# Dilated layer of a two-layer trunk: filler moved from between the weighted sums to between projection, scores, maxima and exponentials of the first head pairs

## The chip, the cores and the metric

The kernel runs on one core of one Trainium2 chip. The metric is device microseconds of one execution of the whole program. Lower is better. A core has TensorE (PE, matmuls and transposes), VectorE (DVE), ScalarE (ACT), GpSimd (POOL) and SyncE (SP, which issues the loads here). "PEld" in a profile is TensorE's loading of the stationary operand, and "PEclk" is the clock that TensorE was granted, as a share of its full 2.4 GHz; the lower of its two levels, 1.2 GHz, reads as 0.50.

## What is computed

The reference is a trunk of two layers over 512 tokens of width 1024. Layer 0 has stick-breaking attention, layer 1 dilated attention; each is followed by a feed-forward block of width 4096 and a gated side input. The change is in the dilated attention alone:

```python
proj = (x @ w_in).reshape(B, S, G, 3, H, HEAD_DIM)        # G = 3 groups, H = 8 heads of 64
for g, (window, dil) in enumerate(((128, 1), (512, 4), (2048, 16))):
    q, k = rope(proj[:, :, g, 0]), rope(proj[:, :, g, 1]); v = proj[:, :, g, 2]
    o, lse = banded_attention(strided(q), strided(k), strided(v), window // dil)
alpha = softmax(stack(lses), axis=0)                       # weights of the three groups
o = einsum('gbsh,gbshd->bshd', alpha, stack(outs))
return o @ w_out
```

All is in 32-bit floats. A product is made of three matmuls on rounded parts (high by high, high by low, low by high).

## The kernel before: how the work is tiled and ordered

**The work of one head pair.** Heads are taken two at a time: pairs 0 to 3. For each pair and each group g there is a *query job* `queries(pr, g)` (L691): the q projection, 8 *steps* of three 128x512 matmuls, then the k projection, 8 steps more. When the last step of a half is reached, its result is turned by the rotary tables on VectorE (L698 to L705: a shuffle, two products, a sum), and after the k half both are split in a rounded high part (ACT) and a low part (VectorE), `qh, ql, kh, kl` (L264, L266). `scores(pr, g)` (L714) is 24 small matmuls, with a masked copy and running maximum of each block on VectorE (L735). When all three groups are scored, `maxima` (L738) transposes the maxima (L743, L745), combines them on ACT and VectorE, and transposes them back (L757); `exps` (L764) makes 16 exponentials on ACT in place in the score tiles `S` (L774). In this document "M-out" is the first set of transposes (L743) and "M-back" the second (L757). Then `attend` (L826) runs the weighted sums: 8 `turn`s (L781: up to four transposes of exponentials, and a split in `th` on ACT, L799, and `tl` on VectorE, L800), 8 `apply`s (L807: matmuls of the values V with th and tl, L820), one `divide` (16 matmuls, L844 and L847, and four reciprocals, L852), and the combination (L874 to L877). Four turns run ahead of the applies.

**The filler.** The order on TensorE is the order in which the program is written out; the other engines are ordered by a planner from priorities (`due`, for instance rope ahead of the split of q and k, that ahead of the scores' copies, those ahead of `tl`). To keep TensorE busy while other engines work, query jobs, and later the values' projection of the last two pairs (`values`, steps of six matmuls), are not run in one piece: they lie in a queue (`Filler`, L118), and the program takes steps from it. `fill(t)` takes steps until their nominal costs (0.65 for a step of a query job, 0.72 for one of the values) cover t; a remainder is carried over. `fill.until(label, then)` takes steps until the job `label` is finished and `then` more of the nominal clock is past. All steps have to run once, so a step that is taken in one place is missing in another.

**Where steps are taken.** The loop over the pairs (L932 to L944) is:

```python
for pr in range(4):
    while pieces and pieces[0][0] == pr:
        fill.until(pieces[0][:2], TUNE["lag"])
        piece()                              # scores of (pr, g)
        fill(TUNE["pgap"])
    fill(TUNE["m0"])
    N = maxima(MM[pr])                       # holds fill(TUNE["m1"]) between M-out and M-back
    late, DD[pr] = exps(SS[pr], N)
    fill(TUNE["m2"])
    if pr < 2:
        attend([pr], TUNE["gap"])
```

Within `attend`, `tick(gap)` (L928) follows each turn ahead and each apply: it takes steps worth `gap`, and then runs the scores of the next pair's next group if its job has been finished for `lag`. So pairs 0 and 1 each have an attend of their own, in which the scores of the next pair lie; pairs 2 and 3 are attended together at the end with their own constant `gap2`, when the queue is empty.

**Buffers.** Tiles of 128x512 come from one pool of 42 (`acts`, L172): the layer's input (16), the rotary tables (2), the four parts of each query job until its scores are done, the eight score tiles of a pair until they have been turned, and the two parts of each pair's output. Score results and turns come from six banks of PSUM (`wb`), projections from two (`mmb`).

Of the kernel before, what the change touches and what calls it, by code (L numbers as in the profile page):

```python
# [25 lines left out]
TUNE = dict(late=4, gap2=1.0, hik=1, lok=0, sqk=1, pieces=4, of=5, og=4, warm=9, wprep=0, s1a=-400, s1b=200, e=25,  # L26
            oev=25, qev=-400, hsplit=-200, vev=50, rope=-800, ttr=-100, exps=200, turn=-50, maxi=-50, comb=-100,
            norm=400, res=-400, resk=2, yev=-50, fev=25, gate=0, fin=-50, fe=2.0, ff=0.0, fg=5.0, qlag=5.0, fa=0.57,
            fb=0.32, slope=0.05, lag=8.0, gap=1.2, m0=6.0, m1=5.5, m2=8.0, p0=5.0, p1=2.0, p2=8.0, hp0=6, hp1=30,
            hps=2, blag=1.5, vlag=0.0, fx=5.5, ahead=4, pgap=0.0, vev1=50)  # L30
NUNIT = 220
BIG = float(2.0 ** 100)
GAINS = ("g_mix_pre", "g_mix_post", "g_ffn_pre", "g_ffn_post", "g_ple")
# [132 lines left out]
def program(tc, ctx, w_dram, x_dram, xs_dram, p_dram, pos_dram, g_dram, c_dram, out_dram):  # L166
# [475 lines left out]
    def dilated(xh, xl, sq, oh, ol, partial, out, prepare):  # L642
        swap = list(range(8, 16)) + list(range(8)) + list(range(16, 32))
        with tc.tile_pool(name="dlw", bufs=1, reuse_waits="tile") as wp:
# [93 lines left out]
            def maxima(M):  # L738

                dve.tensor_max(M[:, 1], M[:, 1], M[:, 2])  # L740
                r0, r1 = wide(), wide()
                for i in range(4):
                    pe.transpose(r1[0:2, i * P:(i + 1) * P], M[:, 1, i, :], ident)  # L743
                for i in range(4):
                    pe.transpose(r0[0:2, i * P:(i + 1) * P], M[:, 0, i, :], ident)  # L745
                fill.clock += 0.9
                m1, m0 = tmp("m1"), tmp("m0")
                with due("maxi"):
                    act.activation(m1[0:2], r1[0:2], AF.Copy)
                    dve.tensor_tensor(sigma(m0[0:2]), sigma(r0[0:2]), cut(m1[0:2]), ALU.max)  # L750
                    dve.tensor_copy(cut(m1[0:2]), sigma(m0[0:2]))
                fill(TUNE["m1"])
                ps = wide()
                for j in range(2):
                    for i in range(4):
                        a = (j * 4 + i) * 2
                        pe.transpose(ps[:, a:a + 2], (m0, m1)[j][0:2, i * P:(i + 1) * P], ident[0:2, 0:2])  # L757
                fill.clock += 0.9
                N = sp.tile([P, 2, 4, 2], F32, name="negmax", bufs=4)
                with due("maxi"):  # L760
                    dve.tensor_scalar(N.rearrange("p a b c -> p (a b c)"), ps[:, 0:16], -0.125, None, ALU.mult)
                return N

            def exps(S, N):  # L764

                done = []
                D = wp.tile([P, 2, 4, 2], F32, name="D")
                for h in range(2):
                    for order in range(2):
                        for i in range(4):  # L770
                            s = S[h, order, i // 2]
                            a, b = (i % 2) * 256 + (P if (i == 0 and order == 0) else 0), (i % 2 + 1) * 256
                            with due("exps"):
                                done.append(act.activation(s[:, a:b], s[:, a:b], AF.Exp, bias=N[:, order, i, h:h + 1],  # L774
                                                           scale=0.125, accum_out=D[:, order, i, h:h + 1]))
                wD = wp.tile([P, 2, 4, 2, 64], F32, name="wD")
                with due("exps"):
                    act.activation(wD, D[:, :, :, :, None].to_broadcast([P, 2, 4, 2, 64]), AF.Copy)
                return done, wD
# [129 lines left out]
            fill = Filler()  # L909
# [8 lines left out]
            def piece():  # L918
                pr, g = pieces.pop(0)
                if pr not in SS:  # L920
                    SS[pr], MM[pr] = {}, sp.tile([P, 3, 4, 2], F32, name="M")
                if g < 2:
                    for n in range(4):
                        SS[pr][n // 2, g, n % 2] = U("S")
                scores(SS[pr], MM[pr], g, *qk.pop((pr, g)))
                fill.clock += 1.7
# [6 lines left out]
            for pr in range(4):  # L933
                while pieces and pieces[0][0] == pr:
                    fill.until(pieces[0][:2], TUNE["lag"])
                    piece()
                    fill(TUNE["pgap"])
                fill(TUNE["m0"])
                N = maxima(MM[pr])
                late, DD[pr] = exps(SS[pr], N)  # L940
                late = late[TUNE["late"]:]
                fill(TUNE["m2"])
                if pr < 2:
                    attend([pr], TUNE["gap"])  # L944

# [12 lines left out]
    def layer(i, h, xh, xl, sq, last):  # L958
# [44 lines left out]
        if i == 0:  # L1003
            stick_breaking(xh, xl, sq, oh, ol, [ple_tile(m, bank, U) for m in range(2)], ple_parts, out)
            later["pool"] = ctx.enter_context(tc.tile_pool(name="wide", bufs=6, space=PSUM, reuse_waits="tile"))
        else:
            outs = {}
            dilated(xh, xl, sq, oh, ol, outs, out, ple_parts)
# [204 lines left out]
```

## Time and profile before

| | |
|---|---|
| median of 3 runs | 1430.84 us (1430.02 to 1432.11) |
| the profiled execution | 1431.45 us, of which the span from first to last instruction 1429.3 us |
| busy: PE, PEld, DVE, ACT | 1401.6, 1181.3, 899.3, 643.4 us |
| share of PE on the chain that ended last | 87% |
| mean granted TensorE clock | 0.995 |

The pairs' part of the dilated attention lies between 765 and 985 us of the span. The chain of waits is the work that ended last, followed back from the end. A timeline row gives start, duration, engine, line, operation, out<-in, shapes and count, and in brackets the engine's idle time just before it and who ended it. Ends of matmuls are modelled and overlap, so distances on PE are taken from start to start.

### The profile page before, as it was taken

Reading aid. Unit: us, or ns where it says so; the run is one execution under the profiler, and the core shown is the slowest. Engines: PE = TensorE matmul, PEld = TensorE weight load, DVE = VectorE, ACT = ScalarE, POOL = GpSimd, SP = SyncE. Lnnn points to the kernel's source line nnn. Section 1 sums busy time; section 2 is a strip of 40 time slices with the busy share of each in tenths; the row PEclk is TensorE's granted clock in tenths of the full one; section 3 lists DMA queues with packets and bytes.
Section 4 is the critical chain, followed back from the end, with each engine's and each line's share of the span. In section 5 each row is a group of like instructions: output and inputs, shape, how many; then the busy total and the mean of one; then the engine's idle time right before and its main releaser. Section 6 shows DMA issues by size and latency. Waiting matters only on the chain.

```text
span 1429.3 us, 18374 instructions
## 1 busy us (share of the span) xinstructions
PE 1401.6 (98%) x7218; PEld 1181.3 (83%) x7218; DVE 899.3 (63%) x1503; ACT 643.4 (45%) x1010; POOL 46.1 (3%) x27
## 2 busy tenths in 40 slices
PE   8999999999999999999999999999999999999998
PEld 7888997888888888887988788899888888888877
DVE  4788886485253453548868888866872444535476
ACT  4788986553232221335552525546632322222353
POOL 0111111000000000000000000000000000000000
PEclk9999999999999999999999999999999999999999
DMA  6344452423232323232522212132323333323321
GB/s 207 104 110 120 111 135 67 138 89 103 89 103 89 103 89 102 90 94 73 167 74 89 74 45 75 59 105 88 89 89 101 91 103 89 102 90 96 96 83 65
DMA packets 45270, 138.86 MB, mean 97 GB/s; under 512 B 5696, under 2 KB 6592, under 8 KB 45184
## 3 DMA queue, kind: packets, MB, share of 16 engines
q1 hardware_dynamic: 45104, 137.43, 31.9%
q8 instruction: 57, 0.93, 0.3%
q0 software_dynamic: 80, 0.26, 0.1%
q14 instruction: 29, 0.24, 0.1%
HBM read 123.51 MB, written 4.19 MB: 89 GB/s over the span
## 4 chain that ended last, share of the span: by engine, by line
PE 87%; DVE 7%; ACT 4%; issue 1%; DMA 1%; SPq 0%; ACTq 0%; DVEq 0%
PE wb L358 17%; PE wb L360 17%; PE wb L362 17%; PE mmb L358 5%; PE mmb L362 5%; PE mmb L360 5%; ACT S L774 1%; DVE wlo L101 1%; PE mmb L421 1%; PE mmb L422 1%; PE mmb L423 1%; PE wb L725 1%; PE z L261 1%; PE z L259 1%; PE z L260 1%
## 5 line engine op out<-in xcount | busy, mean ns | idle before, releaser
L100 ACT ACTIVATE whi<-wraw_t 128x1024 fp32r<-128x1024 f32 (+1 forms) x298 | 228.9, 798 | 440.6 <-PE wb L362 345.7
L101 DVE TENSOR_TENSOR wlo<-wraw_t,whi 128x1024 fp32r<-128x1024 f32 (+1 forms) x310 | 276.1, 911 | 238.7 <-ACT whi L100 235.5
L358 PE MATMUL wb<-nh,whi 128*128 128x512 f32 (+1 forms) x594 | 227.4, 385 | 4.4 <-ACT nh L264 4.4
L360 PE MATMUL wb<-nh,wlo 128*128 128x512 f32 (+1 forms) x594 | 226.4, 384 | 0.0
L362 PE MATMUL wb<-nl,whi 128*128 128x512 f32 x576 | 207.7, 391 | 0.4 <-DVE nl L268 0.4
L358 PE MATMUL wb<-fh,whi 128*128 128x512 f32 x496 | 196.5, 396 | 0.0
L360 PE MATMUL wb<-fh,wlo 128*128 128x512 f32 x496 | 196.5, 396 | 0.0
L362 PE MATMUL wb<-fl,whi 128*128 128x512 f32 x496 | 196.5, 396 | 0.0
L358 PEld LDWEIGHTS wb<-nh,whi 128*128 128x128 f32 x594 | 111.7, 188 | 28.8 <-ACT nh L264 7.0
L360 PEld LDWEIGHTS wb<-nh,wlo 128*128 128x128 f32 x594 | 111.7, 188 | 21.6
L362 PEld LDWEIGHTS wb<-nl,whi 128*128 128x128 f32 x576 | 107.8, 188 | 23.3 <-DVE nl L268 1.3
L362 PEld LDWEIGHTS wb<-fl,whi 128*128 128x128 f32 x496 | 93.3, 188 | 22.4
L358 PEld LDWEIGHTS wb<-fh,whi 128*128 128x128 f32 x496 | 93.3, 188 | 22.4
L360 PEld LDWEIGHTS wb<-fh,wlo 128*128 128x128 f32 x496 | 93.3, 188 | 22.4
L358 PE MATMUL mmb<-nh,whi 128*128 128x512 f32 x248 | 100.1, 404 | 0.0
L362 PE MATMUL mmb<-nl,whi 128*128 128x512 f32 x248 | 97.4, 393 | 0.0
L360 PE MATMUL mmb<-nh,wlo 128*128 128x512 f32 x248 | 97.3, 392 | 0.0
L1103 DVE TENSOR_TENSOR f<-wb,f 128x512 f32<-128x512 f32 (+1 forms) x50 | 33.3, 666 | 73.5 <-PE wb L362 71.1
L1078 DVE TENSOR_TENSOR z<-wb,rrow 128x512 f32<-128x512 f32 x60 | 40.5, 686 | 55.8 <-PE wb L362 55.7
L1081 ACT ACTIVATE fh<-z 128x512 fp32r<-128x512 f32 x64 | 39.9, 631 | 77.3 <-DVE z L1079 77.3
L291 DVE TENSOR_TENSOR acc<-acc,sq 128x512 f32<-128x512 f32 (+1 forms) x74 | 48.8, 659 | 15.6 <-ACT sq L287 15.0
L362 PEld LDWEIGHTS mmb<-nl,whi 128*128 128x128 f32 x248 | 46.9, 189 | 10.2
(818 smaller groups left out, 2600.8 us busy)
## 6 DMA issues: line engine op xcount, KB each, us to landing
wraw_t<-w SPq DMA_DIRECT2D x219, 512.0 KB, 3.6
x<-x SPq DMA_DIRECT2D x8, 256.0 KB, 7.1
h<-xs SPq DMA_DIRECT2D x8, 256.0 KB, 5.9
spill<-h SPq DMA_DIRECT2D x8, 256.0 KB, 2.7
h<-spill SPq DMA_DIRECT2D x8, 256.0 KB, 6.5
out<-h SPq DMA_DIRECT2D x7, 256.0 KB, 2.1
praw<-p SPq DMA_DIRECT2D x4, 256.0 KB, 4.2
wraw_t<-w SPq DMA_DIRECT2D x4, 128.0 KB, 3.5
```

Source lines behind the costliest of these rows:

```text
L100: self.highs.append(self.nc.scalar.activation(hi[:, c], src[:, c], AF.Copy))
L101: self.lows.append(self.nc.vector.tensor_sub(lo[:, c], src[:, c], hi[:, c].bitcast(F32)))
L259: pe.matmul(ps, ah, bh, start=start, stop=False, skip_group_check=True)
L260: pe.matmul(ps, ah, bl, start=False, stop=False, skip_group_check=True)
L261: pe.matmul(ps, al, bh, start=False, stop=stop, skip_group_check=True)
L291: self.adder.tensor_tensor(self.acc[:, cs], self.acc[:, cs], self.sq[:, cs], ALU.add)
L358: pe.matmul(ps[m][:, cs], wh, xh[k][:, cs], start=(k == 0 and cs is not TWO[1]), stop=False, skip_group_check=True)
L360: pe.matmul(ps[m][:, cs], wl, xh[k][:, cs], start=False, stop=False, skip_group_check=True)
L362: pe.matmul(ps[m], wh, xl[k], start=False, stop=(k == nk - 1), skip_group_check=True)
L1078: dve.tensor_mul(z, ps, norm["row"])
L1081: act.activation(a, z, AF.Copy)
L1103: dve.tensor_add(y[m][:, cs], ps, y[m][:, cs])
```

## The change

Constants only, and one term in two calls: `lag` goes from 8.0 to 10.0, `gap` from 1.2 to 1.0, and a new constant `more` of 1.5 is added to the fills before and after `maxima` and `exps` for pairs 0 and 1.

```diff
-            fb=0.32, slope=0.05, lag=8.0, gap=1.2, m0=6.0, m1=5.5, m2=8.0, p0=5.0, p1=2.0, p2=8.0, hp0=6, hp1=30,
-            hps=2, blag=1.5, vlag=0.0, fx=5.5, ahead=4, pgap=0.0, vev1=50)
+            fb=0.32, slope=0.05, lag=10.0, gap=1.0, m0=6.0, m1=5.5, m2=8.0, p0=5.0, p1=2.0, p2=8.0, hp0=6, hp1=30,
+            hps=2, blag=1.5, vlag=0.0, fx=5.5, ahead=4, pgap=0.0, vev1=50, more=1.5)
...
-                fill(TUNE["m0"])
+                fill(TUNE["m0"] + TUNE["more"] * (pr < 2))
                 N = maxima(MM[pr])
                 late, DD[pr] = exps(SS[pr], N)
                 late = late[TUNE["late"]:]
-                fill(TUNE["m2"])
+                fill(TUNE["m2"] + TUNE["more"] * (pr < 2))
```

## Rows read from the trace of the kernel before

**Rows 1.** The page: the span, and the engines' shares of the chain that ended last.
```profile
span 1429.3 us, 18374 instructions
...
PE 87%; DVE 7%; ACT 4%; issue 1%; DMA 1%; SPq 0%; ACTq 0%; DVEq 0%
```

**Rows 2.** Waits of PE, 765 to 985 us: total us, times, longest.
```profile
PE wb L793 <- ACT S L774: 2.4, 2, 1.3
PE wb L725 <- DVE kl L266: 1.9, 1, 1.9
```

**Rows 3.** Windows: length, busy time of each engine, granted clock.
```profile
core 0: us, PE busy (x) PEld busy (x) DVE busy (x) ACT busy (x) POOL busy (x), PEclk, DMA share, GB/s
...
826.00:861.00 35.00, 33.08 (x200) 28.34 (x199) 28.95 (x61) 11.06 (x16) 0.00 (x0) 0.95 0.18 54
...
876.00:911.00 35.00, 35.00 (x247) 30.39 (x244) 30.10 (x86) 11.19 (x18) 0.00 (x0) 1.00 0.16 47
...
959.00:985.00 26.00, 24.42 (x204) 23.33 (x202) 21.11 (x32) 19.25 (x48) 0.00 (x0) 1.00 0.39 123
...
845.50:848.90 3.40, 3.40 (x12) 2.82 (x12) 2.13 (x18) 0.00 (x0) 0.00 (x0) 0.50 0.53 154
```

**Rows 4.** PE timeline: 16 filler steps, scores (0, 2), four steps, M-out of pair 0.
```profile
783.18 0.49 PE L358 MATMUL mmb<-nh,whi 128*128 128x512 f32 x1
...
794.30 0.33 PE L725 MATMUL wb<-kh,qh 64*128 64x128 f32 x2
...
795.79 0.49 PE L358 MATMUL mmb<-nh,whi 128*128 128x512 f32 x1
...
798.65 0.60 PE L743 MATMUL wb<-consts,M 128*2 128x128 f32 x4
```

**Rows 5.** PE timeline: M-back and first turn, pair 0, then pair 1.
```profile
805.11 0.65 PE L757 MATMUL wb<-consts,m 2*128 2x2 f32 x8
...
814.03 0.27 PE L793 MATMUL wb<-consts,S 128*128 128x128 f32 x1
815.56 0.55 PE L793 MATMUL wb<-consts,S 128*128 128x128 f32 x3 [1.25 <-ACT S L774]
...
863.27 0.65 PE L757 MATMUL wb<-consts,m 2*128 2x2 f32 x8
...
872.16 0.27 PE L793 MATMUL wb<-consts,S 128*128 128x128 f32 x1
873.59 0.55 PE L793 MATMUL wb<-consts,S 128*128 128x128 f32 x3 [1.16 <-ACT S L774]
```

**Rows 6.** PE timeline: end of query job (1, 2), its scores, what follows.
```profile
831.64 0.22 PE L820 MATMUL wb<-th,V 128*128 128x128 f32 x1
...
840.99 0.28 PE L725 MATMUL wb<-kh,ql 64*128 64x128 f32 x2
843.19 0.33 PE L725 MATMUL wb<-kl,qh 64*128 64x128 f32 x2 [1.92 <-DVE kl L266]
...
845.40 0.63 PE L358 MATMUL mmb<-nh,whi 128*128 128x512 f32 x1
...
847.96 0.31 PE L820 MATMUL wb<-th,V 128*128 128x128 f32 x1
...
849.25 0.44 PE L358 MATMUL mmb<-nh,whi 128*128 128x512 f32 x1
```

**Rows 7.** DVE timeline: maxima and rope of pair 0; rope and kl of (1, 2).
```profile
798.18 0.17 DVE L740 TENSOR_TENSOR M<-M 128x8 f32<-128x8 f32 x1
...
798.27 0.74 DVE L698 STREAM_SHUFFLE rb<-mmb 128x512 f32<-128x512 f32 x1
...
802.75 0.67 DVE L705 TENSOR_TENSOR rf<-rf,ra 128x512 f32<-128x512 f32 x1
...
833.07 0.74 DVE L698 STREAM_SHUFFLE rb<-mmb 128x512 f32<-128x512 f32 x1
...
842.46 0.67 DVE L266 TENSOR_TENSOR kl<-rf,kh 128x512 fp32r<-128x512 f32 x1
```

## The prediction

> **What bounds the kernel now.** I read the page first: over the span TensorE holds 87% of the chain that ended last, so time is won only where TensorE stands still or runs at its low clock, and lost only where it is made to [rows 1]. Then the waits of TensorE in the pairs' part, 765 to 985 us: the reader is to see two waits for exponentials (2.4 us together) and one for the low part of k, `kl` (1.9 us) [rows 2]. Then the windows: of the two attends with filler in them only the first has a granted clock under 1, and 3.40 us behind the `kl` wait ran at 0.50, that is 1.2 GHz [rows 3]. Last the timelines, to price each of these places and to see what VectorE did before them [rows 4 to 7].
>
> Prices of today's losses, start to start:
> - First turn of pair 0: 815.56 − 814.03 = 1.53, less 0.1 for a transpose's normal distance: 1.4. Pair 1: 873.59 − 872.16 = 1.43, so 1.3 [rows 5].
> - Scores (1, 2): 843.19 − 840.99 = 2.20, less 0.1: 2.1 [rows 6].
> - The low clock: six filler matmuls took 847.96 − 845.40 = 2.56 [rows 6], where two steps take 1.4 elsewhere (16 steps in 794.30 − 783.18 = 11.12, so 0.695 each [rows 4]): 1.1. Eight weighted sums that lay half in the slow stretch lost some 0.4. Together 1.5, and no more than 1.7, half of 3.40 [rows 3].
>
> Sum: 1.4 + 1.3 + 2.1 + 1.5 = **6.3 us**, the most that these places can give.
>
> **The change, part by part.** The work is the same; only the order on TensorE moves, and with it the planner's order elsewhere. I counted steps by walking the filler's arithmetic through the loop; for the order before, the count agrees with the trace (four steps between scores (0, 2) and M-out, for instance: 798.65 − 795.79 = 2.86 [rows 4]).
>
> | place | steps before | after |
> |---|---|---|
> | from a job of pair 0 to its scores | 13 | 16 |
> | scores (0, 2) to M-out | 4 | 6 |
> | M-back to first turn, pairs 0 and 1 | 12 | 15 |
> | within each of the two attends | 21 | 17 |
>
> No DMA moves against its use: a weight block is loaded and prepared by step, not by place, and SP's and POOL's queues keep their order.
>
> *Exponentials to first turn.* Exponentials released the turn 815.56 − 805.76 = 9.8 us after M-back's end in pair 0, and 873.59 − 863.92 = 9.7 in pair 1 [rows 5]. Fifteen steps of 0.695 are 10.4. Pair 1 is then covered by 0.7: 0 left. In pair 0 it is close, and the steps now run into other blocks and splits on ACT, so between 0 and the 1.4 of today; I take 0.4, near the covered end because 10.4 is past 9.8. If the cover is gone, the three transposes behind the first stand, and with them all steps behind on TensorE.
>
> *Scores (1, 2).* Its job now ends before scores (1, 1), not inside the weighted sums. Before, from its last step to its scores were eight steps and some turns and applies, 840.99 − 831.64 = 9.35 us; the row with the wait says that 843.19 − 831.64 = 11.55 was needed [rows 6]. After, there are again eight steps, and besides scores (1, 1) (795.79 − 794.30 = 1.49 [rows 4]), the 16 matmuls of the division and three turns more, less one apply: 9.35 + 1.5 + some 24 small matmuls at the scores' own distance of 1.49/24 = 0.06, 12.3 at the least. What made `kl` late was that its rope began at 833.07 but `kl` ran at 842.46, 9.4 us later, for VectorE work that takes 3 us by itself: reciprocals, low parts of turns and the pair's combination lay in between [rows 7]. Of these, most come later than `kl` in the new order. So 0 of the 2.1 is left, and with no such idle the 1.5 of the clock goes too. Bounds: 0 and 3.6.
>
> *Scores (0, 2) to M-out.* New risk. The k half of job (0, 2)'s successor now ends right before scores (0, 2), and rope goes ahead of the scores' maxima. Before, M was ready 798.35 − 794.30 = 4.05 after the scores began; one rope took 802.75 + 0.67 − 798.27 = 5.15 with a weight block and a step of the maxima in it [rows 4, 7], about 3 alone. TensorE now arrives 1.49 + 6 × 0.695 = 5.7 after the scores' start. M is ready between 4.05 (nothing in the way) and 4.05 + 3 = 7.1: a wait of 0 to 1.4. VectorE had idle time in that stretch, so I take 0.3.
>
> *Score tiles of pair 3.* Counted by last use, the pool of 42 is just full at scores (3, 0) before. After, job (3, 2) is finished before scores (3, 0): 16 + 2 + 12 (three jobs) + 8 (S of pair 2) + 4 (two pairs' outputs) = 42, and the four tiles of scores (3, 0) make 46. They have to wait until (3, 0)'s own q and k are read to the end, so VectorE's copies start up to half a scores block later, 0.75 us, and once more for (3, 1). Between 0 and 1.5, since the banks of scores (3, 1) come free from these copies; I take 0.5, as two of six banks are free without them.
>
> *Shorter attends.* Four steps less is 4 × 0.695 = 2.8 us less of TensorE's work beside about the same work on VectorE, which was busy 28.95 of 35 and 30.10 of 35 us there [rows 3]. The idle 6.05 and 4.9 us are more than 2.8, and one rope, about 3 us, leaves the first attend with its steps. Pair 1's has all three scores of pair 2 ahead of the first apply. I take 0.3 for it. Bounds 0 and 2.8 each.
>
> Sum: −6.3 + 0.4 + 0.3 + 0.5 + 0.3 = **−4.8**. From the profiled execution, 1431.45 (span 1429.3 and 2.15 around it), that is 1426.65. This execution is 0.61 above the median of the runs; on the median 1430.84 − 4.8 = **1426.0**.
>
> One rule speaks against it. Turns are transposes, and in the last attend 16 of them run with hardly any filler, at a granted clock of 1.00 [rows 3]; the only fall in the attends came behind a stand of about 2 us [rows 6]. The Trainium skill, "TensorE: Matmul & The Clock Gate", section "Part 4: PE-mode transpose", says that transposes do not count as work that keeps the clock up as other matmuls do. By that rule attends with less filler would fall to the low clock; this trace does not show it.
>
> **Rivals.**
> 1. *The late `kl` moves to another third group* (same side, little left). Scores (2, 2) now come after 8 steps, two scores and four turns (16 transposes): 8 × 0.695 + 2 × 1.49 + 16 × 0.06 = 9.5 us; scores (3, 2) after ten steps and two scores, 9.9. Pair 0 needed 11.55 [rows 6]. One such wait of 1.6 to 2.1 us with its clock fall costs 3.1 to 3.6: 1426.0 + 3.3 = 1429.3. For: rope, scores' copies and turns' low parts crowd there. Against: the split goes ahead of both in the planner, and pair 1's attend had no such wait before [rows 2].
> 2. *The change doesn't reach the exponentials.* ACT takes a weight block or a split more in the longer stretch, and both turns wait as before, less 0.4 reckoned already: 1426.0 + 2.3 = 1428.3. For: ACT's order is set with other work mixed in. Against: 15 steps exceed both measured releases.
> 3. *The clock falls in the attends for want of filler.* 1.5 each, twice: 1429.0. For: half clock did occur in the first [rows 3]. Against: the last attend at 1.00. The rule of the page named above is the same one.
> 4. *Slower: VectorE sets the length of both attends.* If its idle time there can't be pressed together (it waits for ACT and TensorE in turn), the attends stay as long as they were and the 2.8 us of steps taken out of each are paid in full elsewhere; each stand of that size brings the clock fall seen behind 1.9: 2 × (2.8 + 1.5) = 8.6. 1426.0 + 8.6 = 1434.6. It decides from the point where VectorE's work in such a stretch and the waiting that it can't avoid come to more than 35 − 2.8 = 32.2 us. For: VectorE is at 83 and 86% [rows 3]. Against: 4.9 and 6.05 us idle.
>
> **How the numbers follow.** Forecast 0.58 (its own range 1424.0 to 1427.9: all 6.3 gained and a little more to 1.9 lost again), rival 1 0.15, rival 2 0.09, rival 3 0.06, rival 4 0.12. The range reaches from 1423.5 to 1431.5: below, everything gained, 1424.5, and 1.0 of refill behind the stands that I did not price; above, rivals 1 to 3 whole, and a part of rival 4. A measurement of this kernel can tell about 0.2% from no change, 2.9 us, so faster means below 1427.98. The forecast gives 0.57, rival 2 half of its 0.09, rival 1 a little: faster 0.63. Same: the rest of rivals 1 to 3, 0.26. Slower: 0.11 from rival 4.
>
> **What would show it.** Right: no wait for S at the first turns of more than 0.5 us; none for `kl` at any L725; no stretch at 0.50 between 765 and 985 us; the pairs' part shorter by 4 to 6 us and all else alike. Wrong: a wait for M at M-out over 1 us (the rope ahead of it); L725 waiting for `kl` or for a bank at scores (2, 2), (3, 1) or (3, 2); waits of L820 for `tl` in the first two attends (rival 4); a low clock without a stand before it (rival 3). The prediction fails as a whole if the time is above 1428.

## The result: slower by 10.4 us, and the profile after

| | before | after |
|---|---|---|
| median | 1431.47 us (1430.02 to 1433.03, 4 runs) | 1441.88 us (1440.39 to 1442.40, 4 runs) |
| ratio to before, 95% interval | | 1.0071 (1.0053 to 1.0088) |
| profiled execution, its span | 1431.45, 1429.3 | 1441.73, 1439.6 |
| pairs' part, start to start | 236.0 (748.95 to 984.95) | 246.2 (749.01 to 995.18) |

The pairs' part runs from the last value matmul ahead of the first scores to the last apply. It is 10.2 us longer; nothing was lost elsewhere. The page of after, for [rows 1], shows TensorE with less of the chain that ended last and VectorE with more:

```profile
span 1439.6 us, 18376 instructions
...
PE 83%; DVE 9%; ACT 5%; issue 1%; DMA 1%; SPq 0%; ACTq 0%; DVEq 0%
```

Waits of TensorE in after, 765 to 1000 us, for [rows 2] (total us, times, longest):

```profile
PE wb L725 <- DVE M L735: 4.0, 4, 2.8
PE wb L820 <- DVE tl L800: 2.5, 3, 1.3
PE wb L844 <- DVE M L735: 2.3, 2, 1.7
PE wb L793 <- DVE M L735: 1.5, 1, 1.5
PE wb L743 <- DVE M L740: 1.1, 1, 1.1
PE wb L793 <- DVE tl L800: 0.7, 2, 0.5
PE wb L820 <- ACT th L799: 0.3, 1, 0.3
```

The two kinds of wait that the prediction wanted gone are gone: none for exponentials (S, L774) and none for `kl` (L266). In their place TensorE waits mostly for L735, VectorE's masked copy of a scores block out of PSUM. L725 (scores), L844 (division) and L793 (turn) don't use what that copy writes; they want the PSUM bank that it empties. All waits of the view come to 12.4 us; the same view of before, with its four smaller rows of 0.2 to 1.3 us added to [rows 2], comes to 6.4. So waits explain +6.0.

Windows of after, for [rows 3] (length, busy time of PE, PEld, DVE, ACT and POOL, granted clock, DMA share, GB/s):

```profile
820.80:863.00 42.20, 38.42 (x249) 32.52 (x248) 31.96 (x88) 13.70 (x22) 0.00 (x0) 0.92 0.14 45
885.00:935.00 50.00, 47.08 (x301) 39.43 (x300) 42.37 (x104) 20.66 (x46) 0.00 (x0) 1.00 0.18 53
834.10:837.50 3.40, 3.40 (x18) 3.30 (x17) 1.83 (x12) 0.00 (x0) 0.00 (x0) 0.53 0.01 2
847.70:851.10 3.40, 3.40 (x12) 2.81 (x12) 3.40 (x13) 0.60 (x1) 0.00 (x0) 0.54 0.47 149
943.30:946.70 3.40, 3.40 (x19) 3.40 (x18) 1.90 (x18) 0.00 (x0) 0.00 (x0) 0.53 0.38 136
```

Three stretches of 3.40 us almost wholly at the low level (1.2 GHz) stand where before had one. At the prediction's price of 1.5 us each, an estimate, that is +3.0. Waits and clock make 9.0 of the 10.2; the last 1.2 us are not assigned.

The TensorE timeline of after shows where the waits lie; first the places of [rows 4] and [rows 5]:

```profile
796.40 0.33 PE L725 MATMUL wb<-kh,qh 64*128 64x128 f32 x2
...
803.37 0.60 PE L743 MATMUL wb<-consts,M 128*2 128x128 f32 x4 [1.09 <-DVE M L740]
...
820.77 0.60 PE L793 MATMUL wb<-consts,S 128*128 128x128 f32 x4
...
825.48 0.33 PE L725 MATMUL wb<-kh,qh 64*128 64x128 f32 x2
...
831.39 0.39 PE L820 MATMUL wb<-th,V 128*128 128x256 f32 x1 [1.25 <-DVE tl L800]
832.59 0.66 PE L793 MATMUL wb<-consts,S 128*128 128x128 f32 x4 [0.47 <-DVE tl L800]
...
833.80 0.38 PE L844 MATMUL wb<-consts,wD 128*128 128x128 f32 x1 [0.55 <-DVE M L735]
...
847.03 0.66 PE L793 MATMUL wb<-consts,S 128*128 128x128 f32 x4 [1.51 <-DVE M L735]
...
882.24 0.60 PE L793 MATMUL wb<-consts,S 128*128 128x128 f32 x4
...
897.85 1.16 PE L844 MATMUL wb<-consts,wD 128*128 128x128 f32 x8 [1.74 <-DVE M L735]
...
941.63 0.32 PE L725 MATMUL wb<-kh,qh 64*128 64x128 f32 x1 [2.83 <-DVE M L735]
```

The first turns (820.77, 882.24) are four transposes in one, without a wait. New are 1.09 at M-out; 1.25, 0.47 and then 0.55 at the division behind scores (1, 1), which begin at 825.48; 1.51 behind scores (1, 2); 1.74 behind scores (2, 2); 2.83 within scores (3, 0) and (3, 1). Smaller ones, 0.57 and 0.36, lie within scores (2, 1). VectorE's timeline, for the first row of [rows 7], shows what lies ahead of M-out:

```profile
796.67 0.75 DVE L698 STREAM_SHUFFLE rb<-mmb 128x512 f32<-128x512 f32 x1
...
799.12 1.23 DVE L101 TENSOR_TENSOR wlo<-wraw_t,whi 128x1024 fp32r<-128x1024 f32 x1
800.24 0.30 DVE L735 CUSTOM_DVE_ANT_0 S<-wb,consts 128x128 f32<-128x128 f32 x1
...
803.13 0.18 DVE L740 TENSOR_TENSOR M<-M 128x8 f32<-128x8 f32 x1
```

Three steps of a rope and a weight's low part stand before the copies of scores (0, 2), the rope's sum stands between them and `kl` behind them, and the maxima M are ready at 803.13 + 0.18. The same view behind scores (1, 1):

```profile
827.69 0.74 DVE L698 STREAM_SHUFFLE rb<-mmb 128x512 f32<-128x512 f32 x1
828.32 0.68 DVE L700 TENSOR_TENSOR ra<-mmb,cs 128x512 f32<-128x512 f32 x1
828.91 1.22 DVE L101 TENSOR_TENSOR wlo<-wraw_t,whi 128x1024 fp32r<-128x1024 f32 x1
830.04 0.69 DVE L701 TENSOR_TENSOR rf<-rb,ss 128x512 f32<-128x512 f32 x1
830.64 0.69 DVE L800 TENSOR_TENSOR tl<-wb,th 128x512 fp32r<-128x512 f32 x1
831.24 0.69 DVE L705 TENSOR_TENSOR rf<-rf,ra 128x512 f32<-128x512 f32 x1
831.84 0.69 DVE L800 TENSOR_TENSOR tl<-wb,th 128x512 fp32r<-128x512 f32 x1
832.63 0.69 DVE L266 TENSOR_TENSOR kl<-rf,kh 128x512 fp32r<-128x512 f32 x1
833.24 0.28 DVE L735 CUSTOM_DVE_ANT_0 S<-wb,consts 128x128 f32<-128x128 f32 x1
```

The scores were issued from 825.48 on; their first copy runs at 833.24, 7.8 us later. Ahead of it stand the rope of the half that ended right before the scores, the low part of a weight block, two low parts of turns and `kl`. Until then the banks stay full, and the copies' late place in VectorE's order holds up every user of a bank.

### The profile page after: what moved, and what is told of

It reads as the page before. It is cut to its first block, busy times and chain, and to the rows that moved or that the text cites. A ratio compares the mean times of both kernels' runs of the same rounds, so it can differ in the third digit from the quotient of the medians.

```text
span 1439.6 us, 18376 instructions
## 1 busy us (share of the span) xinstructions
PE 1405.5 (98%) x7218; PEld 1182.9 (82%) x7218; DVE 900.2 (63%) x1503; ACT 643.1 (45%) x1010; POOL 46.1 (3%) x27
## 4 chain that ended last, share of the span: by engine, by line
PE 83%; DVE 9%; ACT 5%; issue 1%; DMA 1%; SPq 0%; ACTq 0%; DVEq 0%
PE wb L358 17%; PE wb L360 17%; PE wb L362 17%; PE mmb L358 4%; PE mmb L362 4%; PE mmb L360 4%; ACT S L774 2%; DVE wlo L101 2%; PE mmb L421 1%; PE mmb L423 1%; PE mmb L422 1%; PE z L261 1%; PE z L259 1%; PE z L260 1%; PE mmb L662 1%
## 5 line engine op out<-in xcount | busy, mean ns | idle before, releaser
L362 PEld LDWEIGHTS mmb<-nl,whi 128*128 128x128 f32 x248 | 47.0, 189 | 10.2
```

Source lines behind the costliest of these rows:

```text
L362: pe.matmul(ps[m], wh, xl[k], start=False, stop=(k == nk - 1), skip_group_check=True)
```

## The experiments

Three theories were tested. **Theory 1** (place): with `lag` 10 the scores of pair 0 and scores (1, 1) come 16 steps after their job, which is exactly two halves, and scores (1, 2) and (2, 2) come 8 steps after it, exactly one, so they are issued right behind the end of another half; that half's rope is ready first, the planner puts it ahead of the copies, and the banks stay held. A half uses up one weight block, so the low part of a new block falls in the same place as the rope, and no run here tells their shares apart. Walking the filler's arithmetic gives each scores block's distance, in steps, from the last end of a half of a query job (groups 0, 1, 2 of pairs 0 to 3); a half that ends right ahead of the scores counts as split for the tiles:

| kernel | pair 0 | pair 1 | pair 2 | pair 3 | most tiles wanted | median us |
|---|---|---|---|---|---|---|
| before | 5, 5, 5 | 7, 1, 0 | 3, 5, 6 | 6, 6, 12 | 42 | 1431.0 |
| after | 0, 0, 0 | 6, 0, 0 | 4, 5, 0 | 2, 2, 10 | 46 | 1441.9 |
| lag 9.5 | 7, 7, 7 | 5, 7, 7 | 3, 4, 7 | 1, 1, 9 | 46 | 1431.5 |
| lag 9 | 6, 6, 6 | 4, 6, 6 | 2, 3, 0 | 0, 0, 13 | 46 | 1438.7 |
| lag 8 | 5, 5, 5 | 3, 5, 0 | 1, 2, 5 | 7, 7, 12 | 43 | 1429.4 |

**Theory 2** (rival 4): 17 steps in an attend are too few for VectorE's work. **Theory 3** (tiles): the pool of 42 is too small at scores (3, 0). Except for the three that start from before, each kernel is after with the edit shown. Ratios are to before on the same chip, with 95% intervals; two kernels are compared by their ratios, 0.1% being 1.4 us.

### One constant back

**Lag back to 8** (`-lag=10.0`, `+lag=8.0`).

> The changed kernel with lag put back from 10.0 to 8.0. By the walk through the filler the attends of pairs 0 and 1 keep their 17 steps, the first turns keep 15 steps behind M-back, and the scores of pair 0 come 5 steps into a job's half again; of the next pairs' scores only (1, 2) and (2, 0) still come within a step behind the end of a half; at most 43 tiles of the pool of 42 are wanted. Theory 1 (scores issued right behind the end of a half: VectorE turns that half and makes a weight block's low part before it copies the scores, and the PSUM banks stay taken): 1428 to 1433 us, waits of TensorE for the copies (L735) under 3 us in all against 7.8. Theory 2 (too few steps in the attends, VectorE sets their length): as the changed kernel, 1439 to 1442. Theory 3 (46 tiles wanted of a pool of 42): some 4 us less than the changed kernel, 1437 to 1438.

Measured 1429.39 us (10 runs), 0.9991 (0.9981 to 1.0002). The slowdown is gone with attends of 17 steps as in after: theory 2 falls as the cause. A first turn waits 1.9 us for exponentials again.

**Gap back to 1.2** (`-gap=1.0`, `+gap=1.2`).

> The changed kernel with gap put back from 1.0 to 1.2. The attends have 20 steps each; scores (0, 0) to (0, 2), (1, 2) and (2, 0) come right behind the end of a half, (1, 1) and (2, 1) one step behind, (3, 0) two; 46 tiles are wanted. Theory 1: hardly better than the changed kernel, 1436 to 1442, waits for L735 again over 5 us. Theory 2: near the kernel before or better, 1427 to 1432. Theory 3: as the changed kernel.

Measured 1433.30 (10 runs), 1.0012 (1.0003 to 1.0021): outside what any of the three theories gave. The walk shows why it tells them apart badly: three or four steps more in each attend also move the scores of pairs 1 to 3. Waits for L735 remain (3.9 us in all), and M-out still waits 1.1.

**The added 1.5 back to 0** (`-more=1.5`, `+more=0`).

> The changed kernel without the new term (more = 0). 12 and 13 steps behind M-back, so the two waits for exponentials come back (up to 2.7 us); attends of 17 steps; scores (1, 1) come 5 steps behind the end of a half, (1, 2) one, (2, 0) two, (2, 1) four, (2, 2) two, (3, 0) one; 42 tiles are wanted. Theory 1: 1431 to 1436. Theory 2: 1440 to 1444. Theory 3: 1437 to 1440.

Measured 1433.19 (10 runs), 1.0017 (1.0005 to 1.0028). TensorE waits 4.7 us for exponentials and 2.4 at M-out, and nowhere for L735. The time lies in the range of theory 1, but with waits for exponentials well over the 2.7 expected: this too moved all places, and turned one kind of wait into another.

### Copies ahead by priority

```diff
-            ttr=-100
+            ttr=-900
```

> The changed kernel with the scores' copies ahead of the rotary turn in the planner (ttr from -100 to -900), the order on TensorE untouched. Theory 1: the waits of TensorE for L735 nearly vanish (under 2 us against 7.8 with those of the turns and divisions behind it), and the time falls to 1428 to 1434; a wait for kl may take a part of it back. Theory 2: the same work on VectorE in the same attends, so 1438 to 1442. Theory 3: the wait at scores (3, 0) stays at 2.8, the time as the changed kernel or 1 to 2 less.

Measured 1441.47 (4 runs), 1.0069 (1.0054 to 1.0084). The expectation of theory 1 missed, but the edit didn't do what it was made for: VectorE's order in the pairs' part changed at one place only (the rope's sum behind scores (2, 2)). The likely reason, which was not tested, is that the priority ranks what is ready at the same time, and the rope is ready first. So this run says nothing for or against theory 1, and an order with the copies ahead of the rope was not tried in any other way. It does show something of the clock: with nearly the waits of after, TensorE ran at the low level from 843.6 to 847.2, 894.8 to 898.4 and 939.2 to 946.2 us (granted 0.53, 0.53 and 0.51), that is behind (1, 2), (2, 2) and (3, 0), and not behind (1, 1).

### One step earlier

**Lag 9.5** (`-lag=10.0`, `+lag=9.5`): 15 steps in place of 16 from a job to its scores. All else that the prediction counted stays: 17 steps in each attend, 15 from M-back to the first turn, 46 tiles wanted.

> The changed kernel with lag 9.5 for 10.0: by the walk, the scores of pair 0 come after 15 steps instead of 16, and nearly every score block comes one step earlier against the halves (7 steps into a half where it was right behind its end), so that its copies are ready before the rotary turn of the next half. Attends (17 steps), first turns (15) and the wanted tiles (46) are those of the changed kernel. Theory 1 (the place against the end of a half): 1428 to 1433 us, the wait at M-out gone, waits for L735 under 3 us against 7.8. Theory 2 (too few steps in the attends) and theory 3 (46 tiles of 42): as the changed kernel, 1439 to 1442.

Measured 1431.53 (10 runs), 0.9999 (0.9989 to 1.0009). One step, 0.695 us of work moved to the other side of twelve blocks, is worth 0.72% (1.0071 against 0.9999), 10.3 us. The views below are of an execution of 1427.91 us. VectorE's timeline of this kernel, whose scores (1, 1) are issued from 821.56 on:

```profile
822.64 0.28 DVE L735 CUSTOM_DVE_ANT_0 S<-wb,consts 128x128 f32<-128x128 f32 x1
...
824.93 0.75 DVE L698 STREAM_SHUFFLE rb<-mmb 128x512 f32<-128x512 f32 x1
```

The first copy now runs 1.1 us after the scores' start, ahead of the rope. Its waits of TensorE, 765 to 1000 us:

```profile
PE wb L725 <- DVE M L735: 3.8, 4, 2.7
...
PE wb L793 <- ACT S L774: 0.8, 1, 0.8
```

The waits at M-out, at the division and at the turns for L735 are gone. What is left at L725, 3.8 us where theory 1 gave under 3, is 2.7 us at scores (3, 1) and three waits of 0.2 to 0.6; the first is the place of theory 3.

**Lag 9** (`-lag=10.0`, `+lag=9.0`): distances 0 at (2, 2), (3, 0) and (3, 1).

> The changed kernel with lag 9.0: 14 steps to the scores of pair 0. Most scores come 2 to 6 steps into a half, but (2, 2), (3, 0) and (3, 1) come right behind the end of one; 17 steps in the attends, 46 tiles wanted. Theory 1: nothing lost in pair 0 and pair 1's scores, a wait for L735 at pair 1's division as in the changed kernel (1.7 us, in all some 3) and one at scores (3, 0) of 2 to 3: 1431 to 1436. Theories 2 and 3: 1439 to 1442.

Measured 1438.66 (4 runs), 1.0055 (1.0037 to 1.0073): more than expected. The two longest waits lie where the table has its zeros, 3.5 us at scores (3, 0) and (3, 1) and 2.1 at the turn behind (2, 2), but their size was not foreseen. Behind each of them TensorE ran at the low level for almost 7 us (0.51 over 891.2 to 898.2 and over 935.4 to 942.4 us), longer in all than in after. That place and tiles meet at (3, 0) may be why the wait is longer there; this was not tested.

### Two tiles more

Two of the four score tiles of (3, 0) get a place of their own, outside the pool of 42:

```diff
-                        SS[pr][n // 2, g, n % 2] = U("S")
+                        SS[pr][n // 2, g, n % 2] = (wp.tile([P, T], F32, name="S", tag="s30", bufs=2)
+                                                    if (pr, g, n % 2) == (3, 0, 0) else U("S"))
```

> The changed kernel with the two score tiles that the first half of scores (3, 0) writes taken from a pool of their own, so that 44 tiles are wanted of the 42 and the copies of (3, 0) can begin after its first half. Theory 3: the wait of 2.8 us at scores (3, 0) and the low clock behind it go, 1437 us or less. Theory 1: the copies stand behind the rotary turn and the weight's low part there, so the wait stays within 1 us of 2.8, and the time within 2 us of the changed kernel.

Measured 1437.33 (4 runs), 1.0039 (1.0024 to 1.0055): 0.32% or 4.6 us under after, 0.3 us above the bound of theory 3, where theory 1 gave 2 us at most. So there are two causes. VectorE's timeline at scores (3, 0), first of after, whose scores begin at 936.51:

```profile
938.87 1.23 DVE L101 TENSOR_TENSOR wlo<-wraw_t,whi 128x1024 fp32r<-128x1024 f32 x1 [0.56 <-ACT whi L100]
940.33 0.69 DVE L266 TENSOR_TENSOR kl<-rf,kh 128x512 fp32r<-128x512 f32 x1 [0.24 <-ACT kh L264]
940.94 0.28 DVE L735 CUSTOM_DVE_ANT_0 S<-wb,consts 128x128 f32<-128x128 f32 x1
```

then with the two tiles, whose scores begin at 936.09:

```profile
937.81 0.28 DVE L735 CUSTOM_DVE_ANT_0 S<-wb,consts 128x128 f32<-128x128 f32 x1
...
938.92 1.21 DVE L101 TENSOR_TENSOR wlo<-wraw_t,whi 128x1024 fp32r<-128x1024 f32 x1
940.05 0.68 DVE L266 TENSOR_TENSOR kl<-rf,kh 128x512 fp32r<-128x512 f32 x1
```

The first copies move from 4.4 us after the scores' start to 1.7, ahead of the weight's low part and `kl`. The wait of 2.83 becomes 0.23, and the low clock at 943 us is gone; two stretches at the low level are left in the pairs' part, behind (1, 2) and behind (2, 2).

**Lag 9.5 and the two tiles together.**

> Lag 9.5 and the two own tiles for scores (3, 0) together: if the loss of the changed kernel has these two causes and no third, the wait of 2.7 us at scores (3, 0) and the low clock behind it go, and nothing of the changed kernel's losses is left but small waits: 1425 to 1429 us. If theory 1 alone were right, as lag 9.5 alone, 1430 to 1433.

Measured 1426.68 (5 runs), 0.9968 (0.9955 to 0.9981), faster than before and after. From after that is 1.03%, 14.7 us; the two edits alone gave 10.3 and 4.6, 14.9 together: they add up. Its waits of TensorE and its two attends with filler:

```profile
PE wb L725 <- DVE M L735: 1.4, 4, 0.5
...
PE wb L793 <- ACT S L774: 0.8, 1, 0.8
```

```profile
818.10:856.00 37.90, 37.13 (x264) 31.66 (x263) 35.51 (x95) 15.54 (x27) 0.00 (x0) 1.00 0.23 70
872.70:909.00 36.30, 35.39 (x252) 30.28 (x250) 34.16 (x92) 14.13 (x22) 0.00 (x0) 1.00 0.19 59
```

**Two tiles at scores (1, 1)** in place of (3, 0) (`(pr, g, n % 2) == (1, 1, 0)`), to see whether the stand there is place alone.

> The changed kernel with two own tiles for the score tiles that the first half of scores (1, 1) writes; TensorE's order is that of the changed kernel. If a shortage of tiles holds these copies back: half of them move ahead of the rest of the turn and of kl, the waits of TensorE behind scores (1, 1) (1.25, 0.47 and 0.55 us in the changed kernel) and the low clock there (1.5) go, 1437 to 1439.5 us. If the place alone does it: within 1 us of the changed kernel, 1441 to 1443.

Measured 1439.34 (4 runs), 1.0059 (1.0042 to 1.0076). By time alone this can't be told from after. The trace can: the waits behind (1, 1) fall from 2.3 us to 1.0, and half of the copies move ahead of the rope's last two steps and `kl` (the first at 830.27, the product L701 at 831.11). The low clock at 834 us is gone, but it is also gone with the copies ranked first, where the waits behind (1, 1) are those of after; here TensorE ran at the low level from 893.8 to 897.4 and 938.2 to 945.2 us, no shorter in all than in after. At (1, 1), then, the place is not all of it: with the copies ranked above the rope (`ttr=-900`) they stayed behind `kl`, with two tiles half of them moved. By last use I had counted 40 of 42 tiles there, so why two more help is not settled.

**The two tiles at both places** (`(pr, g, n % 2) in ((1, 1, 0), (3, 0, 0))`).

> The changed kernel with the two own tiles used by scores (1, 1) and again by scores (3, 0). If both shortages count: the gain of the tiles for (3, 0) alone (4.5 us) and that of (1, 1) add up, 1433 to 1435.5, and what is left over lag 9.5 with tiles (1426.7) is the place, at M-out and at scores (1, 2) and (2, 2). If (1, 1) has no shortage that counts: 1436.5 to 1438, as with the tiles for (3, 0) alone.

Measured 1434.05 (8 runs), 1.0028 (1.0018 to 1.0038), 0.43% or 6.2 us under after, the sum of the two alone (4.6 and 0.12%, 1.7). It stays 0.6%, 8.6 us, above lag 9.5 with its two tiles (0.9968), and its largest waits are those of place, behind scores (2, 2), behind (1, 2) and behind (0, 2). These are blocks of group 2, whose copies write into score tiles that group 1 has taken already (`piece` takes tiles for groups 0 and 1 only), so a missing score tile can't be what holds them:

```profile
PE wb L844 <- DVE M L735: 1.7, 1, 1.7
PE wb L793 <- DVE M L735: 1.5, 1, 1.5
...
PE wb L743 <- DVE M L740: 1.1, 1, 1.1
```

### Fewer steps still, and each constant alone

**Attends of 16 and 15 steps** (`lag=8.5, gap=0.9, m0=5.0, more=2.5`), which leaves no scores of pairs 0 to 2 nearer than 3 steps behind a half's end.

> Constants chosen so that by the walk no scores come within two steps behind the end of a half (lag 8.5, gap 0.9, more 2.5, m0 5.0): 3 to 7 steps into a half everywhere, attends of 16 and 15 steps, 16 steps behind M-back, 43 tiles wanted. Theory 1: no wait for L735 over 1 us, none for exponentials, 1425 to 1429, below the kernel before. Theory 2: fewer steps than ever in the attends, 1440 or more. Theory 3: as with lag 8.0.

Measured 1427.51 (10 runs), 0.9976 (0.9967 to 0.9986): faster with still fewer steps. Theory 2 is refuted outright. No wait for L735 is over 0.7 us; 0.6 for exponentials and 1.1 at M-out are left, the first of which was expected to go.

**Before with one constant of the change**: lag 10, the added 1.5, and gap 1.0.

> The kernel before with lag 10.0 alone. Attends of 21 steps, 12 steps behind M-back, so the waits for exponentials of 1.2 us each stay; four steps to M-out behind scores (0, 2) that come at the end of a half, so a wait at M-out of some 2.4; scores (2, 1), (2, 2) right behind the end of a half, (1, 2), (3, 0), (3, 1) one step behind; 46 tiles wanted. Place and tiles together: 1434 to 1440. Too few steps in the attends (theory 2): as the kernel before, 1429 to 1432.

> The kernel before with the new term alone (more = 1.5). 15 steps behind M-back, attends of 20 steps, scores of pair 0 five steps into a half, the next pairs' 4 to 7, except (2, 2) right behind the end and (3, 0) one step behind, this one inside the attend with steps behind it; 46 tiles wanted for it. Waits for exponentials under 0.8 us, that for kl gone, one wait at pair 1's division of up to 2: 1426 to 1430.

> The kernel before with gap 1.0 alone. 17 steps in the attends; 12 and 13 behind M-back, so the waits for exponentials stay; scores (1, 2) right behind the end of a half, (2, 1) one step behind, the rest 2 to 7; 42 tiles. Place: 1430 to 1434, one wait for L735 or kl of 2 us. Theory 2: 1438 or more.

| ratio to before | neither | added 1.5 | gap 1.0 | both |
|---|---|---|---|---|
| lag 8 | 1 | 0.9979 (0.9969 to 0.9990) | 0.9984 (0.9974 to 0.9993) | 0.9991 |
| lag 10 | 1.0087 (1.0071 to 1.0102) | 1.0012 | 1.0017 | 1.0071 |

Lag 10 alone was worse than expected (1443.70, 4 runs); the other two alone are each a small gain (1427.67, 9 runs, and 1428.85, 10 runs). The added 1.5 came out in its range, but a first turn waited 1.9 us for exponentials where under 0.8 was expected; gap 1.0 came out below its range of 1430 to 1434, without the wait that place gave it. In every column lag 10 is the slower row. The effects don't add, since each constant acts by setting all the places. Two runs set limits to the explanation. With gap 1.0 alone, scores (1, 2) have distance 0 and nothing behind them waits over 0.2 us; they lie behind the attend there, with nine steps up to M-out, so a zero seems to cost only where users of banks follow closely. And with the added 1.5 alone the count of tiles is 46 too, yet L725 waits 0.4 us: its scores (3, 1) come 3.8 us behind (3, 0) (935.93 − 932.10), not right behind. The counts tell where to look, not the price.

## Why the prediction was wrong

Forecast 1426.0 with a range to 1431.5; measured 1441.9. By its own steps:

- **Exponentials to first turn: right in the number, in pair 0 by luck.** Cost 0.4 taken, 0 measured. But the release 9.8 us after M-back, on which 15 steps were reckoned to be enough, isn't fixed. In before with the added 1.5, also with 15 steps:

```profile
806.55 0.65 PE L757 MATMUL wb<-consts,m 2*128 2x2 f32 x8
...
819.71 0.55 PE L793 MATMUL wb<-consts,S 128*128 128x128 f32 x3 [1.93 <-ACT S L774]
```

  That is 819.71 − 807.20 = 12.5 us after M-back's end. ACT had a split of q (L264) ahead of the exponentials, so the first of them began 3.2 us after M-back's end, against 1.4 in after, where that split had run before. With lag 9.5 the release came after 11.4 us, with lag 8 after 12.5.
- **Scores (1, 2): right for `kl`.** No wait for it is left. But behind the same scores TensorE now stands 1.51 for a bank and runs at the low level again, so at the same price of 1.5 most of the 3.6 gained there was lost again.
- **Scores (0, 2) to M-out: mechanism right, size off.** Most of the rope did go ahead of the scores' copies, and so of the maxima. M was ready 803.31 − 796.40 = 6.9 us after the scores began, near the upper bound of 7.1 and not in the middle; the wait was 1.09 where 0.3 was taken.
- **The step that failed: scores inside the attends.** The same rule, rope ahead of the scores' copies, was applied to scores (0, 2) alone. It holds for (1, 2) and (2, 2) as well, and at (1, 1) together with a lack of tiles; behind these scores come turns, applies and the division, which need the banks. The prediction had the 16 steps in its table and the 8 in its text, but it did not draw from them that these are two whole halves and one. Waits there: 1.25 + 0.47 + 0.55 behind (1, 1), 1.51 behind (1, 2), 0.25 + 1.74 behind (2, 2), 5.8 us in all, with two of the three low-clock stretches. The sum had no term for it; lag 9.5 shows 10.3 us for it together with M-out, clock included.
- **Score tiles of pair 3: mechanism right, size off ninefold.** 0.5 taken, bound 1.5; the two tiles won 4.6 us. The bound let the copies start when (3, 0)'s q and k have been read. They did not: by then VectorE's order had a weight's low part and `kl` ahead of them, each with its own wait for ACT, and six banks hold only one and a half scores blocks.
- **Shorter attends: right, rival 4 refuted.** In the first attend of the fastest kernel, again of 17 steps, VectorE was busy 35.51 of 37.90 us, a larger share than rival 4 needed (32.2 of 35), and TensorE was still busy 37.13 of them. The slower side did come, by another mechanism. The sign given for rival 4, a wait of L820 for `tl` in the first attend, did show (1.25), but with lag 9.5 it is gone at the same 17 steps: it was a sign of the place too.
- **Rivals 1 and 2** did not come in after. Of rival 2, ACT with a split more ahead of the exponentials, pair 0 of the kernels above with 15 steps and a late release shows the beginning.
- **Rival 3: refuted.** The clock did fall in the first attend (0.92 over it), but only behind stands. In both attends of the fastest kernel, and in those of 16 and 15 steps, it was 1.00; the latter's windows:

```profile
818.80:856.00 37.20, 36.65 (x261) 31.31 (x260) 34.79 (x93) 14.79 (x25) 0.00 (x0) 1.00 0.21 64
873.30:909.00 35.70, 34.59 (x252) 29.61 (x251) 32.60 (x90) 13.15 (x20) 0.00 (x0) 1.00 0.19 60
```

The Trainium skill, "TensorE: Matmul & The Clock Gate", "Part 4: PE-mode transpose", says that transposes don't count as work that keeps the clock up as other matmuls do. These windows are a weak test of it, since the turns' transposes hold TensorE for only 4.98 of 37.20 and 4.76 of 35.70 us of them. A stronger one is the start of the last attend of the kernel before: from 959.24 to 962.73 us TensorE ran fifteen transposes in 1.80 us and one other matmul of 0.39, and waited 0.29 and 1.02, and the clock stayed at 1.00 [rows 3]; nor did it fall there in the thirteen other kernels whose last attend starts in this way. Here the traces don't agree with the page.

The sum of the losses of before (6.3 us) fits what the runs show: with the two causes removed the kernel gained 4.6 us on before (1430.98 × 0.0032), near the 4.8 forecast, with 0.8 of the first turn still lost. What was wrong is that the change was read as steps taken to better places, while it also put six of the twelve scores blocks in the worst one.

## What to carry to other kernels

When work is moved by a count of steps, find what each block comes right behind, and on each in-order engine write down the order in which the two pieces' followers become ready; a block that empties PSUM late stops every user of a bank, not only its own readers. Apply a mechanism that is priced in one place to all places where the same two pieces meet. Where a pool is full, a tile that comes late is not late by its own wait but by all the work that the planner puts ahead of it in the meantime.

## What was not expected of the hardware

Short stands can cost some 1.5 us more in clock (the prediction's price, an estimate): behind stands of 1.51 and 2.83 us, and behind three that come to 2.27 within 4 us, TensorE ran 3.40 us at a granted 0.53 to 0.54. Behind 1.09 at M-out it did not fall, nor behind the 1.74 of scores (2, 2) (885 to 935 us at 1.00), where in the kernel with tiles at both places it did (0.87 over 887 to 900 us): the length of a stand alone doesn't decide. In the run with the copies ranked first, nearly the same waits brought no fall behind (1, 1), one behind (2, 2), and one twice as long at (3, 0). So the clock's part of a loss that is read from one execution holds for that execution. And a wait for PSUM can name an engine that is not slow: the copies of L735 took 0.27 to 0.42 us each in after, but they came late in VectorE's order.
